# A hybrid decoder step: the projections of both branches as seven-product pairs in the stream

## The chip, the cores and the metric

The kernel runs on one core of one Trainium2 chip. The metric is the device time of one execution in microseconds (us). Engine names: PE is TensorE, DVE is VectorE, ACT is ScalarE, POOL is GpSimd, SP is SyncE, which issues nearly all DMAs.

## What is computed

One layer of a decoder trunk on 1024 prompt tokens, 16 learned meta tokens ahead of them, and 8 single decode tokens, with a model width of 1024. All data are float32.

```
xn   = rmsnorm(h, norm_pre)
proj = xn @ w_in                      # ten sections of 1024 columns
q, fr, i_in, z_a, b_g, c_g, h_c, z_b, gate_a, gate_b = split(proj)
o    = HGRN2 recurrence(silu(q), 1 - f, i_in, log f), per head    # f = lb + (1-lb)*sigmoid(fr)
y_a  = (headnorm(o) * silu(z_a)) @ w_a
y_b  = (b_g * conv3(c_g * h_c) * silu(z_b)) @ w_b
merged = sigmoid(gate_a) * y_a + sigmoid(gate_b) * y_b
out  = merged @ w_o
h    = h + rmsnorm(out, norm_post)
```

The recurrence is exact per token, and the new states of the recurrence and of the convolution are outputs too.

## The kernel before

Activations lie with channels on the partitions and tokens along the free axis, in two halves L and R of 516 or 524 columns (`HY`, `HL`; 512 prompt tokens and a few meta or decode tokens each). A product of float32 precision is made of three matmuls of rounded parts (`mm3`): high weight by high input, high by low, low by high. `split` makes such parts: ACT copies the high part, and DVE (or POOL) subtracts it from the value to give the low part.

**The stream** (`strassen`) computes the input projection. A pair is two output blocks of 128 channels for both halves of the tokens. Of the 2 x 2 blocks of the weights and the 2 x 2 blocks of the input it makes seven products instead of eight. The seven factor sets of the input (`b11`, `b21`, `t2`, `b12`, `t3`, `t4`, `b22`: tiles `s0h` to `s6l`) are made once at the start. Each product j has two steps (chunks of 256 columns and the rest), and each step four `mm3`, so 12 matmuls; a pair has 14 steps. In a step, after the matmuls, the work of the step before is flushed (the copy of a product out of PSUM into `sc`, which must come before the next product accumulates into the same bank; evacuations), then the high part of the weights of product i + 2 is made on ACT (first step) or its low part on DVE (second step). `load` fetches the weights of the next pair in the first three products; `add(p + 1)`, three POOL operations at j = 4, makes the sums of blocks of the next pair's weights; a fourth one (L615) follows within the next pair. All of this is in one order written out by hand (`manual_schedule`): each engine and SP's queue keep the order of the program, and semaphores hold them.

The stream has 39 pairs, numbered from 0: heads and gates up to pair 21, then `u_pair` and `b_pair` of the convolution in turns (pairs 22 to 37), and a last gate pair (38). `weave` puts other work between the steps: the recurrence `hgrn(m)` (42 steps a head), and then `sample_steps`, the decode tokens' recurrence, spread over 14*13 - 6 steps from step 350 on. Results wait in DRAM: `oz_d` (first branch), `ob_d` (second), `ga_d` and `gb_d` (gates).

**The projections of the branches** come after the stream. In its last pair (`tail`) the eight blocks of the first branch's input are loaded and split into the places of factor sets. `y_gemm` is called 16 times, for 8 output blocks of each branch: 8 blocks of input by 4 chunks by `mm3`, 96 matmuls. The gates are multiplied in at the evacuation, and the sum of both branches is `merged`, which stays on the chip. Then the output projection: `out_weight` and `merged_parts` split `w_o` and `merged` for k = 0 to 7, and `out_step` multiplies, 24 matmuls of 512 columns for each k of the first four token blocks.

All tiles of a tag named in `BUFS` have that many buffers, every other tag has one; a new tile of the same tag waits until the last reader of the old one is done, DMAs among them.

Of the kernel before, what the change touches and what calls it, by code (L numbers as in the profile page):

```python
# [19 lines left out]
HL = 524  # L20
HY = 516
# [11 lines left out]
def hybrid_step(ctx: ExitStack, tc: tile.TileContext,  # L33
# [122 lines left out]
    b11, b21, t2, b12, t3, t4, b22 = (factor(j) for j in range(7))  # L156
# [403 lines left out]
    def strassen(pairs, tail):  # L560
# [63 lines left out]
        for p, (_, chunks, _, evac, end) in enumerate(pairs):  # L624
# [3 lines left out]
            if p == len(pairs) - 1:  # L628
                tail["load"]()
            for j in range(7):  # L630
# [13 lines left out]
                for c, ((c0, n), pt) in enumerate(zip(chunks, dst)):  # L644
                    o = pt[:, 0:n]
                    for k in range(4):
                        xh, xl = at(factors[j], k)
                        mm3(o, w[:, 128 * k:128 * k + 128], w[:, 512 + 128 * k:640 + 128 * k],
                            xh[:, c0:c0 + n], xl[:, c0:c0 + n], k == 0 and not onto, k == 3, onto)
# [5 lines left out]
                    if c and p == len(pairs) - 1 and j in tail:  # L655
                        tail[j]()
# [18 lines left out]
    def u_pair(m):  # L675
# [55 lines left out]
        return (sec_of(5, m), sec_of(6, m)), chunks_of(518), (), evac, end  # L731

    def b_pair(m):
# [16 lines left out]
        return (sec_of(4, m), sec_of(7, m)), chunks_of(HY), (), evac, end  # L750

    def gate_pair(sec, m, dst):
# [9 lines left out]
        return (sec_of(sec, m), sec_of(sec, m + 1)), chunks_of(HY), (), evac, lambda: None  # L762

    def context_out():
        for g in range(2):
# [4 lines left out]
            nct = slot("sm", 512)  # L770
# [16 lines left out]
    def sample_steps():  # L787
        loaded = sample_state(0)
        for m in range(8):
# [43 lines left out]
    def place(tag, n, dt=F32R):  # L833

        t = slot(tag, n * NX, dt)
        return [t[:, NX * i:NX * i + NY] for i in range(n)]

    def one(*tags, dt=F32R):
        return [place(t, 1, dt)[0] for t in tags]

    RAWS = ("it", "u", "v", "a", "ee", "f", "k", "kt")

    def load_in(src, ks, tags):

        raws = {}
        for k in ks:
            raws[k] = slot(tags[k % len(tags)], NY)
            sync.dma_start(raws[k], src[k])  # L848
            if src is oz_d:
                pool.tensor_copy(cap(raws[k], 512, [[HY, 2], [1, 4]]), cap(smpz, 8 * k, [[4, 2], [1, 4]]))  # L850
        return raws

    def parts_of(raw, k, parts, hi, lo):
        split(raw[:, 0:NY], hi, lo)
        parts[k] = hi, lo

    def fill(src, parts, ks, places):
        raws = load_in(src, ks, RAWS[:5])
        for k, hi, lo in zip(ks, *places):
            parts_of(raws[k], k, parts, hi, lo)  # L860

    def in_factor(j):
        return place(f"s{j}h", 2), place(f"s{j}l", 2)

    pa, pb = {}, {}
    turn_in, homes = {}, {}

    def at_tail(ks):
        def go():
            for k in ks:  # L870
                if k not in homes:
                    his, los = in_factor(k // 2)
                    homes.update({k + i: (his[i], los[i]) for i in range(2)})
                parts_of(turn_in[k], k, pa, *homes[k])
        return go

    tail = {j: at_tail(ks) for j, ks in enumerate(((0,), (1, 2), (3, 4), (5,), (6,), (7,)))}
    tail["load"] = lambda: turn_in.update(load_in(oz_d, range(8), RAWS))

# [210 lines left out]
    merged = place("s4h", 2, F32) + place("s4l", 2, F32) + place("s5h", 2, F32) + place("s5l", 2, F32)  # L1090

    def y_gemm(w, parts, evac):
        wh, wl = w
        banks = [b() for b in ((hbank,) * 4 if y_gemm.n % 2 else (abank, abank, bbank, bbank))]
        y_gemm.n += 1
        for k in range(8):
            ks = slice(128 * k, 128 * k + 128)
            xh, xl = parts[k]
            for (h, c0, n), pt in zip(CH_Y, banks):
                o = HY * h + c0  # L1100
                mm3(pt[:, 0:n], wh[:, ks], wl[:, ks], xh[:, o:o + n], xl[:, o:o + n], k == 0, k == 7)
        for (h, c0, n), pt in zip(CH_Y, banks):
            evac(slice(HY * h + c0, HY * h + c0 + n), pt[:, 0:n])

    y_gemm.n = 0

    def gate_in(src, m):
        g = slot("x")
        sync.dma_start(g[:, 0:NY], src[m])
        return g  # L1110

    def w_y(w, m):
        return weight(w[0][:, 128 * m:128 * m + 128], lo=("f", "s")[m % 2])

    wa = w_y(w_a, 0)
    ga = gate_in(ga_d, 0)
    for m in range(8):
        w, g = wa, ga
        if m < 7:
            wa, ga = w_y(w_a, m + 1), gate_in(ga_d, m + 1)  # L1120
        else:
            wb, gb = w_y(w_b, 0), gate_in(gb_d, 0)
# [151 lines left out]
```

## Time and profile before

| | us |
|---|---|
| median of 3 runs (1290.95 to 1291.38) | 1290.95 |
| the profiled execution | 1289.68 |
| its span, first to last instruction | 1287.9 |
| PE busy | 1251.0 |
| DVE busy | 852.9 |
| ACT busy | 536.7 |
| POOL busy | 396.1 |

The profile is of one execution. Busy times are of instructions with their latency; matmuls overlap, so that the pace of PE is read from the starts of its instructions. A start is counted from the first instruction of the span. A release is inferred from semaphores.

### The profile page before, as it was taken

To read this page: it belongs to the slowest core of one execution; us is meant where nothing else is said; L and a number is where in the kernel's file an instruction comes from. 1 tells how busy PE (TensorE), PEld (TensorE's weight loads), DVE (VectorE), ACT (ScalarE), POOL (GpSimd) and SP (SyncE) were. 2 spreads that over 40 slices of the span, in tenths; PEclk is the share of its full clock that TensorE was granted. 3 is DMA by queue.
4 is the path that set the end of the run, shared out by engine and by line. 5 is a ranking of instruction groups with operands and counts; after the bars stand their busy time and mean duration, and the time that the engine had idled before them with its cause. 6 is when DMAs were issued, how large, how long until landed. Compare 5 with 4: busy or idle time off the path is not lost. (4 is left out here: it accounts for less than half of the span.)

```text
span 1287.9 us, 25281 instructions
## 1 busy us (share of the span) xinstructions
PE 1251.0 (97%) x10041; PEld 1216.1 (94%) x10041; DVE 852.9 (66%) x1444; ACT 536.7 (42%) x1280; POOL 396.1 (31%) x470
## 2 busy tenths in 40 slices
PE   6899999999999999999999999999999999999997
PEld 5799999999999999999999999999999999999876
DVE  5869597785968768596895776777768424446052
ACT  5555555555545455455443333333335312213031
POOL 5634232332423234232433454444543000000010
PEclk9899999999999999999999999999999999999999
DMA  7011212121221211222114415252428523432041
GB/s 224 9 36 58 69 58 84 52 75 51 68 69 58 83 53 58 61 67 74 53 42 133 124 58 157 75 156 58 124 91 310 178 85 106 156 99 99 2 166 58
DMA packets 146500, 117.11 MB, mean 91 GB/s; under 512 B 6641, under 2 KB 130650, under 8 KB 146382
## 3 DMA queue, kind: packets, MB, share of 16 engines
q1 hardware_dynamic: 145806, 113.40, 28.2%
q8 instruction: 79, 1.29, 0.4%
q0 software_dynamic: 576, 2.10, 0.4%
q14 instruction: 39, 0.32, 0.1%
HBM read 89.48 MB, written 25.96 MB: 90 GB/s over the span
## 5 line engine op out<-in xcount | busy, mean ns | idle before, releaser
L611 DVE TENSOR_TENSOR w<-wq,w 128x512 fp32r<-128x512 f32 x153 | 129.7, 847 | 57.7 <-ACT w L605 56.7
L605 ACT CAST w<-sm 128x512 fp32r<-128x512 f32 x117 | 72.4, 619 | 149.3 <-PE gb L116 123.3
L591 POOL TENSOR_TENSOR sm<-wq 128x512 f32<-128x512 f32 x39 | 67.1, 1721 | 166.1 <-DVE w L611 151.7
L570 ACT COPY sc<-ga 128x256 f32<-128x256 f32 x192 | 71.5, 373 | 105.1 <-PE ga L116 96.8
L611 DVE TENSOR_TENSOR w<-sm,w 128x512 fp32r<-128x512 f32 x117 | 87.0, 743 | 30.1 <-ACT w L605 29.6
L605 ACT CAST w<-wq 128x512 fp32r<-128x512 f32 x156 | 96.8, 621 | 14.5 <-PE ga L116 12.5
L114 PE MATMUL gb<-s1h,w 128*128 128x256 f32 (+3 forms) x344 | 99.2, 288 | 0.8 <-DVE sc L288 0.8
L615 POOL TENSOR_TENSOR sm<-wq,sm 128x512 f32<-128x512 f32 x39 | 60.3, 1545 | 123.1 <-DVE w L611 94.4
L115 PE MATMUL gb<-s1l,w 128*128 128x256 f32 (+3 forms) x344 | 96.8, 282 | 0.0
L114 PE MATMUL gb<-s3h,w 128*128 128x256 f32 (+3 forms) x328 | 94.6, 288 | 1.7 <-DVE sc L288 1.7
L114 PE MATMUL gb<-s6h,w 128*128 128x256 f32 (+3 forms) x328 | 94.5, 288 | 1.6 <-DVE f L288 1.6
L1187 POOL TENSOR_TENSOR st<-st,half 128x1 f32<-128x1 f32 (+1 forms) x9 | 5.0, 551 | 292.9 <-DVE st L1185 290.0
L115 PE MATMUL gb<-s3l,w 128*128 128x256 f32 (+3 forms) x328 | 92.5, 282 | 0.0
L115 PE MATMUL gb<-s6l,w 128*128 128x256 f32 (+3 forms) x328 | 92.4, 282 | 0.0
L116 PE MATMUL gb<-s3h,w 128*128 128x256 f32 (+3 forms) x312 | 88.4, 283 | 1.4 <-DVE w L611 1.2
L116 PE MATMUL gb<-s1h,w 128*128 128x256 f32 (+3 forms) x312 | 88.0, 282 | 0.5 <-DVE w L611 0.5
L116 PE MATMUL gb<-s6h,w 128*128 128x256 f32 (+3 forms) x312 | 88.1, 282 | 0.0
L114 PE MATMUL ga<-s0h,w 128*128 128x256 f32 (+3 forms) x288 | 83.2, 289 | 1.1 <-DVE zs L327 1.1
L115 PE MATMUL ga<-s0l,w 128*128 128x256 f32 (+3 forms) x288 | 81.2, 282 | 0.0
L114 PE MATMUL ga<-s2h,w 128*128 128x256 f32 (+3 forms) x272 | 79.8, 293 | 0.0
L288 DVE TENSOR_TENSOR sc<-gb,sc 128x256 f32<-128x256 f32 (+1 forms) x144 | 60.4, 421 | 27.1 <-PE gb L116 13.6
L593 POOL TENSOR_TENSOR sm<-wq 128x512 f32<-128x512 f32 x39 | 55.5, 1423 | 70.7 <-DVE w L611 67.9
(751 smaller groups left out, 4676.8 us busy)
## 6 DMA issues: line engine op xcount, KB each, us to landing
wq<-in_w_in_dram SPq DMA_DIRECT2D x160, 256.0 KB
oz<-zs SPq DMA_DIRECT2D x16, 258.0 KB
ob<-zs SPq DMA_DIRECT2D x8, 516.0 KB
x<-ga SPq DMA_DIRECT2D x8, 516.0 KB
x<-gb SPq DMA_DIRECT2D x8, 516.0 KB
wq<-in_w_a_dram SPq DMA_DIRECT2D x16, 256.0 KB
wq<-in_w_b_dram SPq DMA_DIRECT2D x16, 256.0 KB
wq<-in_w_o_dram SPq DMA_DIRECT2D x16, 256.0 KB
```

The source lines that it names most:

```text
L114: pe.matmul(pt, wh, xh, start=first, stop=False, skip_group_check=onto)
L115: pe.matmul(pt, wh, xl, start=False, stop=False, skip_group_check=onto)
L116: pe.matmul(pt, wl, xh, start=False, stop=last, skip_group_check=onto)
L288: vec.tensor_tensor(out=out, in0=pt, in1=s, op=ALU.add)
L570: act.copy(held[j][:, cols], o)
L591: pool.tensor_tensor(out=s3, in0=a11, in1=a21, op=ALU.subtract)
L593: pool.tensor_tensor(out=s2, in0=a21, in1=a11, op=ALU.subtract)
L605: act.copy(w[:, 0:512], source(i))
L611: (pool if j in pairs[p][2] else vec).tensor_tensor(out=w[:, 512:1024], in0=source(i), in1=w[:, 0:512].bitcast(F32), op=ALU.subtract)
L615: pool.tensor_tensor(out=s2, in0=raws[p, 0, 1], in1=s2, op=ALU.subtract)
L1187: pool.tensor_tensor(out=rs[0:rows], in0=rs[0:rows], in1=half[0:rows, 0:1], op=ALU.pow)
```

## The change

The projections of both branches become eight more pairs at the end of the stream (pairs 39 to 46, steps `A0` = 546 on; the second branch from `B0` = `A0` + 56). Each pair names its own factor sets (`sets`).

- `exchange` replaces the factor sets one by one: set j is filled anew after its last use in the pair before, in two units of 128 x 1032, by `split` (every third low part on POOL). Units come at steps base + 1 + 1.65 v, base being the start of the pair before the branch's first. Their raw blocks come from DRAM.
- The sums of blocks that some sets need are made by `block_sums`: load two blocks, four subtractions on POOL, write the two sums and the two others to DRAM (`t12`, `t34`). For the first branch it runs within `sample_steps` (m from 4 on), for the second (`b_sums`) at steps `A0` + 6 to `A0` + 31. The decode columns of the first branch are now written into `oz_d` by a DMA each.
- `sample_steps` is spread over 14*11 steps, with 20 steps of `block_sums` more in it.
- `y_pair` multiplies the gates at the evacuation; the first branch's result goes to DRAM (`md`) and is loaded again for the second.
- `context_out` moves from behind the stream to step `A0` + 2.
- The parts of the output projection for k = 0 to 2 are made in the last pair, the rest after it, each k in the place of a factor set. Tiles and banks of the output stage are named anew.

```diff
-        for p, (_, chunks, _, evac, end) in enumerate(pairs):
+        for p, (_, chunks, _, evac, end, sets) in enumerate(pairs):
...
-            if p == len(pairs) - 1:
-                tail["load"]()
...
-                        xh, xl = at(factors[j], k)
+                        xh, xl = at(sets[j], k)
...
-                    if c and p == len(pairs) - 1 and j in tail:
-                        tail[j]()
+                    for f in hooks.pop(14 * p + 2 * j + c, ()):
+                        f()
                     yield
...
+            sync.dma_start(oz_d[m][:].rearrange("p (h c) -> p h c", h=2)[:, :, 512:516],
+                           smpz[:, 8 * m:8 * m + 8].rearrange("p (h c) -> p h c", h=2))
             yield
+            if m >= 4:
+                yield from block_sums(m - 4, oz_d, *sums_a)
...
+    def block_sums(k, src, t12, t34):
+        up, low, t = slot("f", NY), slot("k", NY), slot("s", NY)
+        sync.dma_start(up, src[k])
+        sync.dma_start(low, src[k + 4])
+        yield
+        yield
+        less(t[:, L], up[:, R], up[:, L], pool)
+        less(t[:, R], low[:, R], t[:, L], pool)
+        yield
+        sync.dma_start(t12[k], t)
+        less(up[:, R], low[:, R], up[:, R], pool)
+        less(low[:, L], low[:, L], t[:, R], pool)
+        yield
+        sync.dma_start(t34[k][:, L], up[:, R])
+        sync.dma_start(t34[k][:, R], low[:, L])
+        yield
...
+    def exchange(g0, g1, base, sets, src, t12, t34, tags):
...
+        def load_unit(v):
+            if v < 14:
+                j, i = divmod(v, 2)
+                raw[v] = slot(tags[v % len(tags)], NY)
+                for q in range(2):
+                    sync.dma_start(raw[v][:, HY * q:HY * q + HY], of(j, 2 * i + q))
+
+        def unit(v):
+            j, i = divmod(v, 2)
+            if not i:
+                sets[j] = factor(j)
+            here = [[HL, 2], [1, HY]]
+            split(raw[v].rearrange("p (q c) -> p q c", q=2), cap(sets[j][0], 2 * HL * i, here),
+                  cap(sets[j][1], 2 * HL * i, here), pool if v % 3 == 2 else vec)
+            load_unit(v + len(tags))
+
+        for v in range(len(tags)):
+            at_step(g0 + int(g1 * v), lambda v=v: load_unit(v))
+        for v in range(14):
+            at_step(base + 1 + int(1.65 * v), lambda v=v: unit(v))
...
+    def y_pair(w, m, sets, second):
+        def evac(r, h, c0, n, pt, s):
+            ys = slice(HY * h + c0, HY * h + c0 + n)
+            g = gated_[second, m + r][:, ys]
+            vec.tensor_tensor(out=g, in0=added(pt, s), in1=g, op=ALU.mult)
+            if second:
+                t = merged[m + r][:, ys]
+                vec.tensor_tensor(out=t, in0=t, in1=g, op=ALU.add)
...
+    A0 = 14 * len(stream_of)
+    B0 = A0 + 56
...
+    exchange(A0 - 20, 1, A0 - 14, sets_a, oz_d, *sums_a, ("it", "u", "v", "a", "ee", "kt"))
+    exchange(B0 - 20, 1, B0 - 14, sets_b, ob_d, *sums_b, ("it", "u", "kt", "f", "k"))
+    at_step(A0 + 2, lambda: context_out())
+    b_sums = (x for k in range(4) for x in block_sums(k, ob_d, *sums_b))
+    for i in range(24):
+        at_step(A0 + 6 + int(1.25 * i), lambda: next(b_sums, None))
+    for i, m in enumerate((0, 2, 4, 6)):
+        at_step(A0 - 11 + 14 * i, lambda m=m: gates_in(ga_d, m))
+        at_step(B0 - 11 + 14 * i, lambda m=m: gates_in(gb_d, m))
+        at_step(B0 - 8 + 14 * i, lambda m=m: merged_in(m))
+    for k, g in enumerate((3, 6, 9)):
+        at_step(B0 + 42 + g, lambda k=k: (out_parts(k, 0), out_parts(k, 1)))
...
-    weave(stream, 14 * 13 - 6, sample_steps(), [1] * (8 * N_SAMPLE))
+    weave(stream, 14 * 11, sample_steps(), [1] * (8 * N_SAMPLE + 4 * 5))
     drain(stream)
-    context_out()
     ordered.close()
...
-        y_gemm(w, pa, lambda ys, pt: vec.tensor_tensor(out=merged[m][:, ys], in0=pt, in1=g[:, ys], op=ALU.mult))
...
-        y_gemm(w, pb, ev)
...
+    for k in (3, 4, 5):
+        out_parts(k, 0)
+        out_parts(k, 1)
+    for k, which in ((6, 1), (6, 0), (7, 1), (7, 0)):
+        out_parts(k, which)
```

## Rows read from the trace of the kernel before

**Rows 1.** The page: busy time, share of the span, instructions.

```profile
PE 1251.0 (97%) x10041; PEld 1216.1 (94%) x10041; DVE 852.9 (66%) x1444; ACT 536.7 (42%) x1280; POOL 396.1 (31%) x470
```

**Rows 2.** Windows: stretch, length, busy us by engine, granted clock, DMA share, GB/s.

```profile
700.00:980.00 280.00, 274.85 (x2358) 270.05 (x2358) 202.21 (x351) 101.61 (x235) 128.84 (x157) 1.00 0.39 121
980.00:1002.00 22.00, 21.42 (x178) 20.86 (x178) 19.95 (x27) 17.62 (x31) 3.01 (x5) 1.00 0.86 283
1002.00:1184.00 182.00, 182.00 (x1532) 182.00 (x1531) 75.05 (x160) 40.90 (x74) 0.00 (x0) 1.00 0.38 119
```

**Rows 3.** Timeline of PE: start, length in us, line, operands, columns.

```profile
979.94 0.28 PE L114 MATMUL ga<-s0h,w 128*128 128x256 f32 x1
982.78 0.28 PE L114 MATMUL gb<-s1h,w 128*128 128x256 f32 x1
...
1001.89 0.36 PE L114 MATMUL ga<-s0h,w 128*128 128x256 f32 x1
...
1184.71 0.40 PE L114 MATMUL ga<-s2h,it 128*128 128x512 f32 x1
```

**Rows 4.** Waits between 690 and 1000 us: total us, times, longest.

```profile
ACT w L605 <- POOL sm L591: 6.9, 3, 2.8
PE gb L114 <- DVE sc L288: 2.5, 2, 1.7
PE gb L116 <- DVE w L611: 1.7, 4, 0.5
```

**Rows 5.** Groups from 700 us on: busy us, mean ns, idle before.

```profile
L611 DVE TENSOR_TENSOR w<-wq,w 128x512 fp32r<-128x512 f32 x51 | 43.1, 845 | 6.9 <-ACT w L605 6.6
L288 DVE TENSOR_TENSOR sc<-gb,sc 128x256 f32<-128x256 f32 x19 | 7.9, 417 | 0.5 <-ACT sc L570 0.4
L91 DVE TENSOR_TENSOR s1l<-v,s1h 128x1032 fp32r<-128x1032 f32 x2 | 2.4, 1224 | 0.0
L91 DVE TENSOR_TENSOR f<-wq,w 128x512 fp32r<-128x512 f32 x16 | 10.3, 684 | 0.0
L605 ACT CAST w<-wq 128x512 fp32r<-128x512 f32 x54 | 33.6, 622 | 12.7 <-PE ga L116 10.8 <-issue 2.0
L570 ACT COPY sc<-ga 128x256 f32<-128x256 f32 x21 | 7.8, 373 | 12.5 <-PE ga L116 10.2 <-DVE w L611 2.3
L90 ACT CAST s1h<-v 128x1032 fp32r<-128x1032 f32 x2 | 2.1, 1054 | 0.1
```

**Rows 6.** The same groups on POOL, from 690 us on.

```profile
L615 POOL TENSOR_TENSOR sm<-wq,sm 128x512 f32<-128x512 f32 x14 | 23.1, 1650 | 49.9 <-DVE w L611 22.7 <-ACT w L605 12.5 <-ACT sc L570 7.1
L591 POOL TENSOR_TENSOR sm<-wq 128x512 f32<-128x512 f32 x13 | 22.1, 1702 | 32.1 <-DVE w L611 25.2 <-DMA wq<-in_w_in_dram 6.8
L593 POOL TENSOR_TENSOR sm<-wq 128x512 f32<-128x512 f32 x14 | 20.4, 1458 | 10.2 <-DVE w L611 7.5 <-DVE it L694 2.1
```

**Rows 7.** Timelines of DVE and POOL around 946 us: start, length.

```profile
946.42 1.22 DVE L804 TENSOR_TENSOR u<-u,v 128x1024 f32<-128x1024 f32 x1
...
946.59 2.21 POOL L591 TENSOR_TENSOR sm<-wq 128x512 f32<-128x512 f32 x1 [3.82 <-DVE w L611]
951.63 1.29 POOL L593 TENSOR_TENSOR sm<-wq 128x512 f32<-128x512 f32 x1 [1.13 <-DVE w L611]
```

**Rows 8.** A load in the chain, a wait for a small copy, DMA rate.

```profile
986.51 3.89 DMA it<-ob
...
DVE w L1235 <- DMA s<-w: 2.1, 1, 2.1
...
976.00:977.00 1.00, 1.00 (x11) 1.00 (x10) 1.00 (x2) 0.22 (x1) 1.00 (x1) 1.00 1.00 409
```

**Rows 9.** Windows near the start: columns as in rows 2.

```profile
48.00:50.00 2.00, 0.13 (x2) 0.00 (x0) 1.97 (x2) 0.59 (x1) 1.92 (x2) 1.00 0.00 0
50.00:52.00 2.00, 1.15 (x6) 1.18 (x7) 2.00 (x2) 0.03 (x1) 1.92 (x3) 0.53 0.04 8
56.00:58.00 2.00, 2.00 (x15) 1.84 (x14) 2.00 (x2) 0.34 (x1) 2.00 (x2) 0.77 0.02 4
```

More of the change, by code (lines that the diff above doesn't have):

```diff
@@ L841, in hybrid_step @@
[L841 to L877, printed above, removed]
@@ L878, in hybrid_step, with sums_of @@
-    tail["load"] = lambda: turn_in.update(load_in(oz_d, range(8), RAWS))
+            if m >= 4:
+                yield from block_sums(m - 4, oz_d, *sums_a)
+    def sums_of(name):
+        return [[kept.tile([128, NY], F32, name=f"{name}{i}{k}", tag=f"{name}{i}{k}") for k in range(4)] for i in range(2)]
+    sums_a, sums_b = sums_of("ta"), sums_of("tb")
+    L, R = slice(0, HY), slice(HY, NY)
+    def block_sums(k, src, t12, t34):
[14 more added lines that the diff above has]
+        yield
@@ new lines, in hybrid_step, with gates_in, merged_in, end @@
+    md = spilled("md")
+    gated_ = {}
+    merged = {}
+    MERGED = ("v", "a", "ee", "s", "it", "u", "kt", "f")
+    def gates_in(src, m):
+        for r, tag in ((0, "x"), (1, "zs")):
+            gated_[src is gb_d, m + r] = g = slot(tag, NY)
+            sync.dma_start(g, src[m + r])
+    def merged_in(m):
+        for r in range(2):
+            merged[m + r] = slot(MERGED[m + r], NY)
+            sync.dma_start(merged[m + r], md[m + r])
+    def y_pair(w, m, sets, second):
[6 more added lines that the diff above has]
+                vec.tensor_tensor(out=t, in0=t, in1=g, op=ALU.add)
+        def end():
+            if not second:
+                for r in range(2):
+                    sync.dma_start(md[m + r], gated_[second, m + r])
+        return (w[0][:, 128 * m:128 * m + 128], w[0][:, 128 * m + 128:128 * m + 256]), chunks_of(HY), (), evac, end, sets
@@ L880, in hybrid_step, with out_parts @@
+    homes = {}
+    def out_parts(k, which):
+        if k < 7:
+            if k not in homes:
+                homes[k] = factor(k)
+            hi, lo = (t[:, 1024 * which:1024 * which + 1024] for t in homes[k])
+        else:
+            hi, lo = (slot(t, 1024, F32R)[:, 0:1024] for t in ("x", "zs"))
+        (merged_parts if which else out_weight)(k, hi, lo)
     gates = [gate_pair(8, m, ga_d) for m in (0, 2, 4, 6)] + [gate_pair(9, m, gb_d) for m in (0, 2, 4, 6)]
@@ L1105, in hybrid_step @@
[L1105 to L1122, printed above, removed]
-        y_gemm(w, pa, lambda ys, pt: vec.tensor_tensor(out=merged[m][:, ys], in0=pt, in1=g[:, ys], op=ALU.mult))
-        if m == 1:
-            fill(ob_d, pb, (0, 1), in_factor(6))
-        if m == 3:
-            fill(ob_d, pb, (2, 3), (one("zs", "k"), one("zs", "kt")))
@@ L1152, in hybrid_step @@
-    for m in range(8):
-        w, g = wb, gb
-        if m < 7:
-            wb, gb = w_y(w_b, m + 1), gate_in(gb_d, m + 1)
-        def ev(ys, pt):
-            vec.tensor_tensor(out=g[:, ys], in0=pt, in1=g[:, ys], op=ALU.mult)
-            vec.tensor_tensor(out=merged[m][:, ys], in0=merged[m][:, ys], in1=g[:, ys], op=ALU.add)
-        y_gemm(w, pb, ev)
-        if m in (1, 2):
-            (h0, h1), (l0, l1) = in_factor(m + 1)
-            out_weight(2 * m - 2, h0, l0)
-            out_weight(2 * m - 1, h1, l1)
-        if m in (3, 4):
-            merged_parts(m - 3, *one(*(("it", "v"), ("a", "ee"))[m - 3]))
-        if m == 5:
-            merged_parts(2, *place("s4h", 2))
```

103 lines of the change are left out of this document (41 added, 62 removed).

## The prediction

> **What bounds the kernel now.** I read the busy shares first: TensorE (PE) is busy 97% of the span [rows 1]. Three stretches tell more [rows 2]: the u and b pairs with the sample steps beside them (700 to 980 us), the last pair of the stream (980 to 1002) and the two plain projections (1002 to 1184). In the last one PE has no gap and the granted clock is 1.00, while VectorE (DVE) works 75 of 182 us, ScalarE (ACT) 41 and GpSimd (POOL) not at all. So the projections are bound by PE's instruction count, with much room beside it. In the stretch before, DVE is at 72%, POOL at 46%, and PE loses 5 us of 280. Its waits name the operands of the next products and the emptying of PSUM [rows 4]. So in the seven-product form PE stays the bound, but what feeds it runs in order and close behind.
>
> **What the removed products are worth.** The plain projections run from 1001.89 to 1184.71 us [rows 3]: 182.8 us for 16 calls of 8 x 4 x 3 = 96 matmuls, 1536 in all, or 119.0 ns each. In seven-product form they are 8 pairs of 7 products of 2 x 4 x 3 = 24 matmuls, 1344 in all, with chunks of the same 256 and 260 columns. One product of the stream takes 982.78 - 979.94 = 2.84 us [rows 3], 118.3 ns a matmul, so the form changes the count and not the pace. I take 119.0 ns: 1344 of them are 159.9 us, **22.9 us less**, if PE never waits. A pair is then 20.0 us, and one of its 14 steps (12 matmuls) 1.43 us.
>
> The Trainium skill (TensorE: Matmul & The Clock Gate, Back-to-back issue gap) gives an isolated gap of columns / 2.4 + 2.5 ns, 110 ns for 258 columns; by it, as an estimate, the 192 matmuls would be worth 21.1 us. The trace shows 119 ns.
>
> **What is added, and what hides it.** Per pair DVE gets 7 low parts (0.68 us alone, 0.85 with POOL beside them), 6 additions and 8 multiplications of some 0.42 us, and in the second branch 8 additions more [rows 5]: 11 to 15 us of 20. ACT gets 7 high parts and 6 copies, 0.62 and 0.37 us [rows 5], 6.6 us. POOL gets four operations of block sums at 1.4 to 1.7 us [rows 6], some 6 us. All of that fits under 20 us of PE. Moving the context output costs nothing: its transposes are the same. The gates and the merged sums that go through DRAM are loaded a pair ahead.
>
> *Sums of blocks of the first branch* (in the sample steps, four times four subtractions on POOL) now stand in a stretch where POOL also carries the pairs' sums and half of u. Once, in pair 30, they come between the pair's sums and the last products of u, whose buffer the next pair's first copy wants. I count 1 us, between 0 and 4 (once in each of the four blocks). *The sample steps* are pressed from 176 steps into 154; the waits there were 2.5 and 1.7 us [rows 4], and I take 1 us more, between 0 and 4. Neither can be a gain: they add work and take room.
>
> *Sums of blocks of the second branch* (b_sums) are the step that matters. They are written into the steps 6 to 31 behind the first projection pair, 6.25 steps (8.9 us) for each of four blocks. Their three tiles (f, k, s) have one buffer each, so a block's loads wait until the previous block's results have been written to DRAM. POOL takes its instructions in order: while a subtraction waits for a load, the sums of the next pair's weights (add) wait behind it, ACT's cast of that sum waits in turn, and behind the cast on ACT the copy that frees the pair's first bank. Prices: a subtraction of 516 columns 1.29 us alone [rows 7] and 1.4 to 1.7 on average beside a busier DVE [rows 6]; I take 1.45, since DVE is less busy here. A load of 516 KB takes 3.9 us among others [rows 8], and alone 2.1 us (the small copy of the same rows) and 1.3 us of transfer at 409 GB/s, 3.4 us; a write of half as much is then 2.7 us. From the first projection pair's start, in us:
>
> - block 0: POOL is through with an exchange unit and L615 at about 6.2; a weight quarter waits for that on SP, and behind it stand two gate loads and the block's loads, issued at about 8.3, landed 13.0 behind those transfers; two subtractions to 15.9; the sums of pair 40 (3 x 1.45 and gaps) to 20.4; two subtractions to 23.3; written 26.0
> - block 1: landed 29.4; two to 32.3; the pair's second sum (L615) to 33.8; two to 36.7; written 39.4
> - block 2: landed 44.1 (behind two gate loads, 1.3 us more); four subtractions to 49.9; only then the sums of pair 41, which stand behind them in POOL's program, to 54.4
>
> The third product of pair 41 needs that sum, a cast (0.62) and a low part (0.75): 55.8 us. PE would be there after 32 steps, 45.8 us (0.3 later for L615 in block 1). It waits 9.7 us. After an almost idle stretch of PE the granted clock stood at 0.5 for about 6.8 us (from 0.53 in the stretch from 50 to 52 us and 0.77 in that from 56 to 58, PE busy 0.13 of 2 us ahead of it) [rows 9], the lower of the two levels (1.2 GHz), which costs 3.4 us of work at 2.4. Together 0.3 + 9.7 + 3.4 = **13.4 us**. With 1.29 us for a subtraction and no queue for the loads the wait is 4 us and the clock may hold; with 1.72 it is 15 us and the clock, 18.4 us. Bounds 4 and 18.4.
>
> *The exchanges in place*: 14 units of 128x1032, ten on DVE (1.22 us alone) and four on POOL (two times 1.29), with 1.05 us of ACT each [rows 5, 7]. A set is read last at step 2j+1 of its pair and wanted 13 steps later, while its two units come at about 3.3j+1 and 3.3j+2.7: the last has 4 steps, 5.7 us, to spare. At the first exchange DVE has 7 x 0.7 + 6 x 0.42 + 6 units = 15 us of 20; the pair that stood there before, with eight splits in it, lost 0.6 us as well between 980 and 1002 us [rows 2]. I take 0.5 us, between -0.6 and 3. At the second, over two pairs: 14 low parts at 0.8, ten units at 1.45 (between alone and the slow ones), 36 operations of 0.42 at the evacuations (28, and 8 additions of the second branch) take 41 us of 40. DVE falls behind; the operands have about two steps of slack. I take 2.5 us, between 0 and 8.
>
> *The last pair* has the splits of the output projection in it. Four casts (2.5 us) come on ACT between the two halves of the fifth product's copy, and the sixth product needs the second half: 1 to 3 us, I take 1.5. The output projection itself keeps its matmuls; its first three k are split by then, and each later k takes DVE some 3 us, while PE's 24 matmuls of it have twice a product's columns, so about twice its 2.84 us.
>
> **Sum:** -22.9 + 13.4 + 1 + 1 + 0.5 + 2.5 + 1.5 = -3.0 us. The profiled execution took 1289.68 us (span 1287.9) and lies 1.3 us under the median of 1290.95; the difference is taken to the median: **1288 us**.
>
> **Rivals.** *The block sums stay hidden* (chance 0.25). The copies and POOL run ahead of the order of the steps, since only semaphores hold them; if loads and writes return sooner than I took, or pair 41's sums get past, the 13.4 us shrink to 2 or less. For it: PE lost 5 us in 280 with POOL at 46%, and ACT waited for POOL's sums 6.9 us in three places, none over 2.8 us [rows 4]. Against it: 12 subtractions, 2 sums, three loads and two writes are one chain, and nothing overlaps in it. Time: 1290.95 - 22.9 + 6.5 = 1275, from 1272 to 1279.
>
> *DVE and POOL exclude each other, and the second exchange decides* (0.22, the other side). A POOL subtraction that started 0.17 us after a DVE operation with two SBUF inputs took 2.21 us, against 1.29 alone, while the DVE operation kept its 1.22 [rows 7]; DVE's low parts take 0.85 against 0.68 [rows 5]. If every such pair of operations is served one after the other, the two pairs of the second exchange hold 9.6 (low parts) + 12.2 (units) + 8.4 (20 multiplications and additions from SBUF) on DVE and 10.3 (pair sums) + 10.3 (units) on POOL: 51 us of work in 40. With some 3 to 4 us of slack PE then waits 7 us there, 2 at the first exchange (45 in 40), and the block sums go to their 1.72 us end: -22.9 + 18.4 + 2 + 2 + 7 + 1.5 = +8, 1299 us, from 1293 to 1304. It decides from where DVE's two-input operations and POOL's operations together pass the time of the pair.
>
> The Trainium skill (SBUF — State Buffer, SBUF: two separate sides) says the same as a rule: the port pair that DVE and GpSimd share is an exclusive lock for the whole instruction, and the loser fully blocks. The trace agrees in the instance above.
>
> *The count does not fall, or a product takes longer*: excluded by the pace of a product in the stream; 0.
>
> **How the numbers follow.** Forecast 0.53, with its own range of 1279 to 1296 (the block sums between their bounds, and a little for the small terms); hidden 0.25; port 0.22. A measurement of this kernel tells changes of about 0.2% (2.6 us) from none: faster means under 1288.4, slower over 1293.5. Of the forecast 0.29 lies below, 0.17 between and 0.07 above; of the port rival 0.21 is slower and 0.01 between. Faster 0.25 + 0.29 = 0.54, same 0.18, slower 0.28. The range leaves out the ends of the two rivals: 1274 to 1300.
>
> **What would show it.** PE's instructions fall by 192, and the stretch from the last gate pair to the output projection gets shorter than 182.8 us by what is left. The forecast is right if PE has one gap of 5 to 13 us in the third projection pair, released by a low part or copy behind POOL's sums, with POOL waiting for DMA before its subtractions and the granted clock at 0.5 behind the gap. If PE's longest wait there is under 2 us, the chain is wrong and the time is near 1275. If DVE is at 95% and more over the two pairs of the second exchange, with PE waiting for units or low parts, the port decides. Waits in the sample steps of over 8 us would make the small terms wrong.

## The result, and the profile after

The changed kernel takes **1312.08 us** (median of 4 runs, 1310.55 to 1312.5), the kernel before 1291.07 beside it: ratio **1.016, 95% interval 1.0143 to 1.0178**, slower by 21 us. The prediction was 1288, with a range of 1274 to 1300.

The page's first lines (busy us, share of the span, instructions) answer to [rows 1]:

```profile
span 1308.8 us, 25416 instructions
...
PE 1243.9 (95%) x9849; PEld 1203.7 (92%) x9849; DVE 940.0 (72%) x1520; ACT 578.3 (44%) x1364; POOL 504.7 (39%) x534
```

PE has 192 instructions less, as worked out, and yet a longer span: its idle time rose from 36.9 to 64.9 us. The windows cut the run at the first matmul of a pair (columns as in [rows 2]): pairs 25 to 37 (u and b pairs, sample steps), 38 (last gate pair, first exchange), 39 to 41 (first projection, b_sums), 42 to 44 (second exchange), 45 and 46.

```profile
702.37:990.64 288.27, 276.35 (x2338) 269.43 (x2337) 211.46 (x351) 101.96 (x235) 146.60 (x166) 1.00 0.46 140
990.64:1019.57 28.93, 22.90 (x170) 22.69 (x169) 16.27 (x20) 15.43 (x27) 10.93 (x6) 0.88 0.72 234
1019.57:1094.07 74.50, 65.35 (x514) 64.50 (x513) 49.11 (x68) 25.28 (x49) 43.40 (x29) 0.93 0.76 259
1094.07:1164.36 70.29, 63.76 (x507) 62.32 (x505) 63.69 (x88) 32.23 (x54) 31.66 (x18) 0.98 0.77 271
1164.36:1205.79 41.43, 41.43 (x343) 40.87 (x341) 35.55 (x74) 22.96 (x51) 6.49 (x5) 1.00 0.46 153
```

Against the kernel before (277.65 us for pairs 25 to 37, 21.95 for pair 38, 0.8 of it context output, that now stands in pair 39; 182.8 for the plain projections), and with 20.0 us for a pair that never waits (pair 45 took 20.1), the 21 us come out so: -22.8 arithmetic, +10.6 in pairs 25 to 37, +8.4 first exchange (7.8 in pair 38, 0.6 in pair 39), +13.1 in pairs 40 and 41, +10.3 second exchange (9.5 in pairs 42 and 43, 0.8 in 44), +1.4 in the last two. After the stream both kernels take 103 us.

**The chain of block sums** is there as written down. POOL's timeline (start, length, idle before):

```profile
1035.89 1.30 POOL L219 TENSOR_TENSOR s<-f 128x516 f32<-128x516 f32 x1 [4.07 <-DMA f<-ob]
...
1067.93 1.28 POOL L219 TENSOR_TENSOR s<-f 128x516 f32<-128x516 f32 x1 [8.38 <-DMA f<-ob]
1069.29 1.30 POOL L219 TENSOR_TENSOR s<-k,s 128x516 f32<-128x516 f32 x1
1070.56 1.27 POOL L219 TENSOR_TENSOR f<-k,f 128x516 f32<-128x516 f32 x1
1071.79 1.27 POOL L219 TENSOR_TENSOR k<-k,s 128x516 f32<-128x516 f32 x1
1073.02 1.26 POOL L591 TENSOR_TENSOR sm<-wq 128x512 f32<-128x512 f32 x1
1074.36 1.26 POOL L592 TENSOR_TENSOR wq<-wq 128x512 f32<-128x512 f32 x1
1075.69 1.26 POOL L593 TENSOR_TENSOR sm<-wq 128x512 f32<-128x512 f32 x1
```

Pair 41's sums end 57.4 us behind the start of pair 39 (54.4 was worked out). PE's wait of 7.1 us ends at 1077.93, in the third product of pair 41. The waits of PE and ACT show who stood behind them (us in total, times, longest):

```profile
PE h L114 <- ACT sc L570: 7.1, 1, 7.1
...
PE ga L114 <- ACT sc L570: 2.0, 1, 2.0
```

```profile
ACT w L605 <- POOL sm L593: 18.4, 2, 14.1
ACT w L605 <- POOL sm L615: 8.6, 2, 5.8
```

**The first exchange** has a wait that the prediction did not name. ACT's copy of PSUM into sc stands until a gate's two writes to DRAM have read that sc buffer (there are two buffers). ACT had the gate's halves ready at 998.57 and 1000.36; SP issued their writes at 1002.40 and 1004.44, behind loads of the exchange, and into queues that were full (DMA share 0.97 to 1.07 from 1002 to 1010 us). Of the second write's delay 4.1 us are SP's order and 6.3 us the time from issue to release. ACT's waits, SP's timeline, ACT's timeline, and windows of 2 us:

```profile
ACT sc L570 <- DMA gb<-sc: 6.9, 1, 6.9
```

```profile
1002.40 0.80 SPq L757 DMA_DIRECT2D gb<-sc  x1
1003.29 1.05 SPq L876 DMA_DIRECT2D v<-ta  x2
1004.44 0.39 SPq L757 DMA_DIRECT2D gb<-sc  x1
```

```profile
1010.78 0.37 ACT L570 COPY sc<-ga 128x256 f32<-128x256 f32 x1 [6.94 <-DMA gb<-sc]
```

```profile
1008.00:1010.00 2.00, 0.00 (x0) 0.00 (x0) 0.00 (x0) 0.00 (x0) 1.26 (x1) 1.00 1.07 400
1010.00:1012.00 2.00, 0.79 (x3) 0.79 (x4) 0.42 (x1) 1.22 (x2) 1.26 (x1) 0.51 0.98 373
1012.00:1014.00 2.00, 2.00 (x12) 2.00 (x11) 0.11 (x1) 2.00 (x5) 1.81 (x1) 0.50 0.12 44
```

PE and ACT idle, the DMA share at 1, and behind it the granted clock at 0.5, the level of 1.2 GHz, as near the start of the kernel before [rows 9]. Between 1000 and 1110 us it stood there for 20.4 us (from 1010.0, 1057.8, 1074.9 and 1105.6), each time late in a wait of PE or just behind one. PE worked for 16.2 us of that, at half the pace, so about 8 us of the excess are lost to it (an estimate).

**The second exchange** shows DVE and POOL by turns. Timeline of DVE, then of POOL:

```profile
1105.29 0.43 DVE L912 TENSOR_TENSOR x<-sc,x 128x260 f32<-128x260 f32 x1
...
1115.70 0.42 DVE L288 TENSOR_TENSOR sc<-gb,sc 128x260 f32<-128x260 f32 x1
1116.15 2.20 DVE L912 TENSOR_TENSOR zs<-sc,zs 128x260 f32<-128x260 f32 x1
1118.27 0.41 DVE L912 TENSOR_TENSOR zs<-ga,zs 128x256 f32<-128x256 f32 x1
...
1121.12 2.19 DVE L912 TENSOR_TENSOR x<-sc,x 128x256 f32<-128x256 f32 x1
```

```profile
1114.65 3.41 POOL L91 TENSOR_TENSOR s2l<-it,s2h 128x1032 fp32r<-128x1032 f32 x1
1119.76 3.26 POOL L91 TENSOR_TENSOR s4l<-f,s4h 128x1032 fp32r<-128x1032 f32 x1 [1.70 <-ACT s4h L90]
```

The multiplication of 260 columns took 0.43 us at 1105.29, where POOL was idle; [rows 7] had one meeting, in which POOL was the one that waited. At 1116.15 it took 2.20 and ended 0.3 us behind POOL's unit (1118.06); at 1121.12 it was the same. The sum at 1115.70, one operand in PSUM, took its 0.42 inside POOL's unit. The Trainium skill (SBUF — State Buffer, SBUF: two separate sides) has this distinction too: beside DVE's operations in a 2-port mode it names those with two SBUF inputs, against a GpSimd operation that reads SBUF. The trace agrees: in the groups from 1094 to 1144 us the multiplications of two SBUF operands average 874 to 1312 ns, the sums with one operand in PSUM 414 to 417.

```profile
L912 DVE TENSOR_TENSOR x<-sc,x 128x256 f32<-128x256 f32 x4 | 5.0, 1252 | 0.1
L912 DVE TENSOR_TENSOR x<-sc,x 128x260 f32<-128x260 f32 x4 | 3.5, 874 | 0.1
...
L288 DVE TENSOR_TENSOR sc<-gb,sc 128x260 f32<-128x260 f32 x6 | 2.5, 417 | 0.0
```

### The profile page after: what moved, and what is told of

It is laid out like the page before. It is cut to its first block, busy times and chain, and to the rows that moved or that the text cites. A ratio compares the mean times of both kernels' runs of the same rounds, so it can differ in the third digit from the quotient of the medians.

```text
span 1308.8 us, 25416 instructions
## 1 busy us (share of the span) xinstructions
PE 1243.9 (95%) x9849; PEld 1203.7 (92%) x9849; DVE 940.0 (72%) x1520; ACT 578.3 (44%) x1364; POOL 504.7 (39%) x534
## 5 line engine op out<-in xcount | busy, mean ns | idle before, releaser
L611 DVE TENSOR_TENSOR w<-wq,w 128x512 fp32r<-128x512 f32 x185 | 162.5, 878 | 66.3 <-ACT w L605 65.2
L611 DVE TENSOR_TENSOR w<-sm,w 128x512 fp32r<-128x512 f32 x141 | 112.4, 797 | 48.7 <-ACT w L605 48.2
L591 POOL TENSOR_TENSOR sm<-wq 128x512 f32<-128x512 f32 x47 | 79.0, 1680 | 172.3 <-DVE w L611 153.8
L605 ACT CAST w<-wq 128x512 fp32r<-128x512 f32 x188 | 116.7, 622 | 29.4 <-PE ga L116 21.4
L114 PE MATMUL gb<-s1h,w 128*128 128x256 f32 (+3 forms) x376 | 109.0, 290 | 2.0 <-DVE sc L696 1.8
L114 PE MATMUL gb<-s3h,w 128*128 128x256 f32 (+3 forms) x376 | 109.2, 291 | 1.6 <-ACT w L605 1.1
L116 PE MATMUL gb<-s3h,w 128*128 128x256 f32 (+3 forms) x376 | 107.4, 286 | 3.2 <-DVE w L611 3.1
L114 PE MATMUL gb<-s6h,w 128*128 128x256 f32 (+3 forms) x376 | 108.3, 288 | 2.3 <-DVE f L288 1.5
L116 PE MATMUL gb<-s1h,w 128*128 128x256 f32 (+3 forms) x376 | 106.3, 283 | 2.8 <-DVE w L611 2.8
L116 PE MATMUL gb<-s6h,w 128*128 128x256 f32 (+3 forms) x376 | 106.0, 282 | 0.0
L288 DVE TENSOR_TENSOR sc<-gb,sc 128x256 f32<-128x256 f32 x192 | 80.5, 420 | 35.2 <-ACT sc L570 18.1
L593 POOL TENSOR_TENSOR sm<-wq 128x512 f32<-128x512 f32 x47 | 65.3, 1389 | 74.6 <-DVE w L611 73.5
L114 PE MATMUL ga<-s5h,w 128*128 128x256 f32 (+3 forms) x288 | 85.3, 296 | 8.5 <-ACT sc L570 8.0
L115 PE MATMUL ga<-s5l,w 128*128 128x256 f32 (+3 forms) x288 | 83.3, 289 | 0.4 <-DVE s5l L200 0.4
```

Source lines behind the costliest of these rows:

```text
L114: pe.matmul(pt, wh, xh, start=first, stop=False, skip_group_check=onto)
L115: pe.matmul(pt, wh, xl, start=False, stop=False, skip_group_check=onto)
L116: pe.matmul(pt, wl, xh, start=False, stop=last, skip_group_check=onto)
L288: vec.tensor_tensor(out=out, in0=pt, in1=s, op=ALU.add)
L591: pool.tensor_tensor(out=s3, in0=a11, in1=a21, op=ALU.subtract)
L593: pool.tensor_tensor(out=s2, in0=a21, in1=a11, op=ALU.subtract)
```

## The experiments

All are edits of the changed kernel. Stage lengths in us, from the same marks in PE's timeline of one profiled execution each; the time is the median of the runs. Not every difference is an effect: pairs 42 to 44 take 69.2 to 70.6 us in the kernels whose edits leave the second branch's sums and both exchanges alone, pairs 39 to 41 take 74.5 to 77.4 without an edit of their own, and the kernel before, run beside each, had medians of 1289.3 to 1291.1.

| kernel | pairs 25-37 | 38 | 39-41 | 42-44 | time |
|---|---|---|---|---|---|
| changed | 288.3 | 28.9 | 74.5 | 70.3 | 1312.1 |
| samp176 | 292.1 | 29.1 | 76.4 | 69.8 | 1315.2 |
| aahead | 291.5 | 28.1 | 77.0 | 70.2 | 1316.9 |
| aphase | 295.5 | 29.0 | 76.8 | 69.2 | 1320.5 |
| asumtiny | 279.7 | 28.2 | 77.4 | 70.6 | 1304.6 |
| aheaddve | 282.0 | 29.1 | 77.4 | 70.6 | 1308.1 |
| gateaway | 287.6 | 20.4 | 82.9 | 70.2 | 1310.0 |
| gateaway2 | 290.9 | 20.4 | 81.1 | 70.0 | 1311.2 |
| bahead | 289.0 | 28.9 | 64.0 | 74.9 | 1305.0 |
| exdve | 288.1 | 29.1 | 74.4 | 66.1 | 1307.5 |
| comboB | 288.1 | 21.4 | 64.2 | 68.8 | 1293.1 |
| combo1 | 293.1 | 20.4 | 64.0 | 69.8 | 1296.8 |
| combo2 | 293.6 | 20.4 | 64.0 | 70.0 | 1297.7 |
| combo3 | 281.6 | 20.4 | 64.0 | 69.1 | 1284.6 |
| combo4 | 282.9 | 20.4 | 73.7 | 65.5 | 1291.6 |
| combo5 | 282.7 | 20.4 | 64.0 | 72.2 | 1289.4 |

### Pairs 25 to 37: room, loads, place, or POOL's work

samp176:

```diff
-    weave(stream, 14 * 11, sample_steps(), [1] * (8 * N_SAMPLE + 4 * 5))
+    weave(stream, 14 * 13 - 6, sample_steps(), [1] * (8 * N_SAMPLE + 4 * 5))
```

> The sample steps and the block sums of the first branch are woven over 176 steps of the stream again, as before the change, and not over 154; all else is as in the changed kernel. Theory A (room: the 108 small steps are pressed too close): pairs 25 to 37 fall from 288.3 us towards 279, the whole to about 1303 us. Theory B (POOL stands behind a load and a subtraction order, whatever the room): the waits only move, pairs 25 to 37 stay within 285 to 290, the whole 1308 to 1313 us. I hold B the likelier.

Room gives nothing back: 292.1 us, and 1315.2 for the whole, are over the ranges of both theories. The pressed sample steps are not the cause; B's "only moves" is nearer.

aahead:

```diff
-                yield from block_sums(m - 4, oz_d, *sums_a)
+                waiting.append(block_sums(m - 4, oz_d, *sums_a, ahead=3))
```

with a generator around sample_steps that takes one step of the waiting sums beside each step of the next sample, and again in 176 steps.

> The first branch's block sums run beside the next sample's steps and not between two samples: their loads are issued three small steps earlier before the first subtraction, and the whole has 176 steps of the stream again. Theory A (POOL stands at a subtraction whose load is under way, 7.2 us at 872, and what is queued behind it comes late): pairs 25 to 37 fall from 288.3 us (292.1 with 176 steps alone) to about 281, the whole to about 1305 us. Theory B (the 23 us of subtractions themselves on POOL are too much beside the pair's sums and u): they stay at 286 or more, the whole over 1309 us.

291.5 us. Theory A falls: pairs 31 and 33 do get shorter (from 26.0 and 27.9 to 23.9 and 24.8), but pairs 35 to 37 take 73.0 us and not 63.3. Against samp176 (292.1, also 176 steps) the new place is worth 0.6 us, which is within the spread.

aphase:

```diff
+    a_sums = [block_sums(k, oz_d, *sums_a) for k in range(4)]
+    for k, g in enumerate((14 * 32 + 12, 14 * 33 + 8, 14 * 34 + 12, 14 * 36 + 12)):
+        for i, s in enumerate((0, 2, 4, 7, 9, 10)):
+            at_step(g + s, lambda k=k: next(a_sums[k], None))
```

> The first branch's block sums, the same loads, subtractions and writes, are tied to steps of the pairs: they start at the end of a u pair (after its products have left) and end before the end of the next one, in the pairs 33, 33 to 34, 35 and 37; the 88 steps of the samples keep their 154 steps of the stream. Theory A (only where the subtractions fall matters: at the end of a u pair they stand ahead of u's products on POOL, which the convolution's taps on ACT wait for, and the casts of the weights stand behind these): pairs 31 and 33 fall from 26.0 and 27.9 to under 23 us, pairs 25 to 37 from 288.3 to some 280, the whole to about 1304 us. Theory B (their amount on POOL and in the DMA queues matters, wherever they stand): pairs 25 to 37 stay at 286 or more.

295.5 us (pairs 31 and 33 fall to 23.2 and 24.7, pairs 35 and 37 now take 30.6 and 27.2): the place is not the cause either. But the trace shows what the sums do. DVE's and POOL's timelines in pair 35:

```profile
931.53 1.24 DVE L722 TENSOR_SCALAR zs<-cx,vecs 128x8 f32<-128x8 f32 x1
932.81 1.33 DVE L723 SCALAR_TENSOR_TENSOR zs<-cx,vecs,zs 128x8 f32<-128x8 f32 x1
934.17 1.20 DVE L724 SCALAR_TENSOR_TENSOR zs<-x,vecs,zs 128x8 f32<-128x8 f32 x1
```

```profile
931.01 1.73 POOL L219 TENSOR_TENSOR s<-f 128x516 f32<-128x516 f32 x1
932.82 1.29 POOL L219 TENSOR_TENSOR s<-k,s 128x516 f32<-128x516 f32 x1
934.07 1.27 POOL L219 TENSOR_TENSOR f<-k,f 128x516 f32<-128x516 f32 x1
935.31 1.28 POOL L219 TENSOR_TENSOR k<-k,s 128x516 f32<-128x516 f32 x1
```

Three operations of 8 columns end with one POOL subtraction each, and two of them last as long as it does. The same kind takes 0.22 us in the changed kernel's groups:

```profile
L722 DVE TENSOR_SCALAR zs<-cx,vecs 128x8 f32<-128x8 f32 x7 | 1.5, 221 | 0.0
```

So POOL's work itself became the suspect.

asumtiny:

```diff
-        less(t[:, L], up[:, R], up[:, L], pool)
-        less(t[:, R], low[:, R], t[:, L], pool)
+        n = 8 if src is oz_d else HY
+        P, Q = slice(0, n), slice(HY, HY + n)
+        less(t[:, P], up[:, Q], up[:, P], pool)
+        less(t[:, Q], low[:, Q], t[:, P], pool)
```

and the other two alike, into t.

> The first branch's block sums subtract 8 columns of each half and not 516; their loads, writes and places in the order are as in the changed kernel (the first projection's sums of blocks are thereby left out of the computation, the blocks as loaded stand in their place). Theory A (the 23 us of POOL's subtractions, behind which POOL's other work and, at the port they share, DVE's operations with two SBUF operands come late): pairs 25 to 37 fall from 288.3 to 280 to 282 us, the whole to about 1305. Theory B (the loads, the small write of smpz and SP's order, which are all still there): 286 or more.

Theory A holds: with all loads and writes still there, 279.7 us, so 8.6 of the 10.6 us hang on POOL's subtractions. One thing goes with them: the writes no longer wait for the subtractions, for which SP, in order, had waited 21.7 us in the changed kernel (first line below). This run doesn't part the two; in aheaddve below, SP still waits for subtractions. POOL's busy time in the stretch falls from 146.60 to 125.66, DVE's from 211.46 to 203.40 with the same 351 operations:

```profile
SPq L851 <- POOL s L219: 21.7, 4, 6.8
```

```profile
703.06:982.75 279.69, 274.65 (x2338) 269.13 (x2337) 203.40 (x351) 102.17 (x235) 125.66 (x166) 1.00 0.47 145
```

aheaddve:

```diff
-        less(t[:, L], up[:, R], up[:, L], pool)
+        eng = vec if src is oz_d else pool
+        less(t[:, L], up[:, R], up[:, L], eng)
```

and the other three alike, run beside the next sample as in aahead, in 154 steps.

> The first branch's block sums on DVE, where a subtraction of two SBUF operands over 516 columns takes half of POOL's time, with the loads three small steps ahead, in the 154 steps of the changed kernel. Theory A (DVE and POOL take turns, so 10 us of DVE weigh less than 23 of POOL): pairs 25 to 37 fall from 288.3 to 281 to 284. Theory B (DVE's own load decides): 289 or more.

Theory A holds, 282.0 us: the same 16 subtractions cost 6.3 us less on the engine that is busier, and DVE's busy time does not rise (211.12 us, now for 367 operations). The place changed with the engine; by aahead against samp176 the place is worth 0.6 us of it. The whole falls by 4.0 us, since pairs 39 to 41 take 2.9 more, as in asumtiny.

```profile
703.40:985.39 281.99, 276.21 (x2338) 270.46 (x2337) 211.12 (x367) 101.75 (x235) 126.44 (x150) 0.99 0.46 143
```

### Pair 38: the gates' writes

gateaway:

```diff
+                if away and s is not None:
+                    if (r, h) not in outs:
+                        outs[r, h] = slot(("f", "k", "s")[r + h], HY)
+                    out = outs[r, h][:, c0:c0 + n]
```

> The last gate pair puts its gates into the free tiles f, k and s instead of back into the two sc buffers, so that the copies of PSUM into sc don't wait for the writes to DRAM. Theory A (the writes stand in SP's queue behind the exchange's loads and hold sc): pair 38 falls from 28.9 to some 21.5 us, the clock stays up at 1010 us, the whole to about 1304 us. Theory B (the exchange's units themselves, DVE and the full DMA queues hold the pair): ACT's wait goes, another takes its place, pair 38 stays at 27 us or more, the whole within 2 us of 1312.

Pair 38 falls to 20.4 us, so theory A holds for the pair: the writes are as late behind the pair's start as before (11.5 and 13.7 us; before 11.8 and 13.8), but the copies into sc no longer wait for them. But pairs 39 to 41 take 8.4 us more, and the sum stays. ACT's waits name a part of it:

```profile
ACT w L605 <- POOL sm L593: 23.6, 3, 16.6
...
ACT s L775 <- DMA gb<-s: 4.4, 1, 4.4
```

gateaway2:

```diff
-    at_step(A0 + 2, lambda: context_out())
+    at_step(A0 - 17, lambda: context_out())
```

> The last gate pair's gates in f, k and s as in gateaway, and the context output 19 steps of the stream earlier, so that its copies (tiles f and s) don't stand behind the gates' writes. Theory A (in gateaway the gain of 8.5 us was lost to ACT's 4.4 us wait of the context copy for a write, which this takes away): pair 38 stays at 20.4, pair 39 falls from 29.6 to 21 or 22, pairs 38 to 41 from 103.4 in the changed kernel to about 95 us, the whole to about 1304 us. Theory B (the loads of the block sums come no sooner, so that the chain behind pair 41 eats what is won): pairs 38 to 41 stay at 101 us or more, the whole 1309 us or more.

Pairs 38 to 41 take 101.5 us: theory B. The 4.4 us are gone, and the chain of block sums swallows the rest: POOL's sums for pair 41 end at 1077.6 (in the changed kernel 1077.0), though pair 39 began 5.5 us earlier. (Of pair 38's gain 0.9 us went to the context output, now in pair 37; pairs 25 to 37 took 2.6 us more in all, the rest without a cause shown.) What PE wins ahead of the chain, it waits for in it (9.3 us once, before 7.1):

```profile
PE h L114 <- ACT sc L570: 9.3, 1, 9.3
```

### Pairs 40 and 41: the block sums of the second branch

bahead, the generator cut to its core:

```diff
+            got[k] = [slot(t, NY) for t in (("f", "k", "s"), ("v", "a", "ee"))[k % 2]]
...
+            sync.dma_start(sums_b[1][k][:, L], up[:, R])
+            sync.dma_start(sums_b[1][k][:, R], low[:, L])
+            if k < 2:
+                loads(k + 2)
```

> The block sums of the second branch use two sets of tiles by turns (f, k, s and v, a, ee), each block's loads are issued a block ahead, and POOL's four subtractions of a block come in two places two small steps apart. Theory A (the chain of load, subtraction, write, load on one set of tiles stands on POOL before the pair's sums): POOL has no wait for DMA over 2 us there, PE's 7.1 us wait in pair 41 goes, pairs 40 and 41 fall from 53.1 to 41 or 42 us, the whole to about 1300 us. Theory B (it is the amount of POOL's work beside DVE): the two pairs fall by 4 us at most, the whole stays over 1307 us.

Theory A holds for the two pairs: they take 41.6 us, with the same 16 subtractions, and PE's longest wait there is 0.9 us. POOL no longer waits for the blocks' loads (its waits for other DMAs, up to 3.1 us, stay). But pair 39 takes 1.0 us more, and pairs 42 and 43 take 54.2, 4.7 more: the second exchange takes back part of the gain, so that the whole falls to 1305.0 and not to 1300.

```profile
PE ga L116 <- DVE w L611: 0.9, 1, 0.9
```

### Pairs 42 to 44: DVE's load, or turns with POOL

exdve:

```diff
-                  cap(sets[j][1], 2 * HL * i, here), pool if v % 3 == 2 else vec)
+                  cap(sets[j][1], 2 * HL * i, here), vec)
```

> All 14 units of each exchange have their low parts on DVE, none on POOL. Theory A (DVE and POOL exclude each other): in the two pairs of the second exchange POOL gives back 10.3 us and DVE takes 4.9 more, the work that can't overlap falls from 51 to some 45 us, pairs 42 and 43 fall from 49.5 to about 45 us, the whole to about 1306 us. Theory B (DVE's own load decides, POOL beside it is free): DVE has 46 us of work in 40, the two pairs take 53 us or more, the whole about 1315 us.

Theory A holds: pairs 42 and 43 fall from 49.5 to 45.3 us, and DVE, with more to do (57 operations against 54), is busy for less time (42.78 against 46.01 us). Some 1.7 of the 4.2 us are the clock, which no longer falls at 1105.6 (an estimate, half of its 3.4 us). First exdve, then the changed kernel:

```profile
1094.77:1140.05 45.28, 42.17 (x339) 40.72 (x338) 42.78 (x57) 25.85 (x40) 14.04 (x9) 1.00 0.93 330
```

```profile
1094.07:1143.57 49.50, 43.35 (x338) 42.11 (x337) 46.01 (x54) 25.74 (x40) 26.44 (x14) 0.97 0.87 309
```

### Together

comboB is gateaway2, bahead and exdve.

> Three edits together: gates in f, k, s with the earlier context output, the second branch's block sums on two sets of tiles, the exchanges' low parts all on DVE. Theory A (the three causes stand apart and their prices add: 8, 11.5 and 4.2 us): 1288 to 1290 us. Theory B (the second exchange is a bound of its own, and what is won ahead of it is given back there as in bahead, where pairs 42 and 43 took 4.7 us more): 1294 us or more, with pairs 42 and 43 at 50 us or more.

1293.1 us: between the two, nearer to theory A. 19 of the 23.7 us add up; pair 39 starts 7.3 us earlier than in the changed kernel, and with the chain gone that start is kept. Pairs 42 to 44 stay at 68.8. combo1 adds aahead, combo2 aphase:

> The three edits of comboB and the first branch's block sums as in aahead. If the prices add up, comboB's time less what aahead wins (some 7 us if POOL's wait for the loads was the cause): about 1282 us, faster than before. If aahead wins nothing, this is within 2 us of comboB.

> comboB's three edits and the first branch's block sums placed as in aphase. By theory A of aphase 1293.1 - 8 = about 1285 us, 0.3% faster than before; by theory B 1292 to 1295 us, slower than before.

Neither helped (1296.8 and 1297.7 us, 3.7 and 4.6 over comboB), in line with aahead and aphase alone. combo3 has comboB's edits and aheaddve's.

> comboB (1293.1 us) with the first branch's block sums as in aheaddve. By theory A of aheaddve 1286 to 1289 us; by B 1294 or more.

**1284.6 us, ratio to the kernel before 0.9958 (0.9943 to 0.9974)**: the change with these four edits is faster than the kernel before, by 5.4 us. The second exchange still costs some 9 us (69.1 for three pairs of 20.0). combo4 moves the sums of the weights too:

```diff
-                pool.tensor_tensor(out=s3, in0=a11, in1=a21, op=ALU.subtract)
+                eng = vec if p > 41 else pool
+                eng.tensor_tensor(out=s3, in0=a11, in1=a21, op=ALU.subtract)
```

and the other three operations alike.

> combo3 with the sums of the weights' blocks (three of four operations for the pairs from 42 on, the fourth from 41 on) on DVE as well, so that POOL is idle in the second exchange. Theory A (taking turns at the port): 4 operations of 1.3 us on POOL become 4 of 0.7 on DVE, some 2.5 us a pair less of work that can't overlap, pairs 42 to 44 fall from comboB's 68.8 to some 64 us, 4 to 5 us under combo3. Theory B (DVE's load): 2.7 us more DVE work a pair, 71 us or more, slower than combo3.

Pairs 42 to 44 fall to 65.5 us, near theory A's 64, but pair 41 loses 9.7, and the whole is 7.0 us over combo3 and not 4 to 5 under it. DVE, in order, now stands behind the load of a weight quarter where POOL stood before. Pairs 42 and 43 in combo3, then in combo4:

```profile
1068.83:1116.52 47.69, 44.18 (x339) 42.22 (x337) 40.21 (x56) 25.31 (x40) 14.89 (x10) 0.96 1.01 358
```

```profile
1080.44:1125.23 44.79, 42.27 (x338) 41.87 (x337) 40.39 (x65) 25.66 (x40) 0.00 (x0) 0.96 0.90 314
```

That turns at the port made the gain is not shown. PE's wait in pair 41 may give the second exchange a head start: behind such a wait pairs 42 to 44 are shorter in other kernels too, 66.1 us in exdve against 68.8 without it in comboB, 70.3 in the changed kernel against 74.9 in bahead. And with POOL idle the two pairs still take 4.8 us more than 40, with the clock at 0.96: turns are not all that bounds them. combo5 begins one pair later (p > 42):

> combo4 with the weights' sums on DVE one pair later (from pair 43 on, the fourth operation from pair 42 on). In combo4 the first of them put DVE behind a weight quarter that was still under way (5.5 us at 1074), PE then waited 7.15 us. Theory A (turns at the port in the second exchange, and that one wait apart): pair 41 falls from 29.8 to 20.1, pairs 42 to 44 stay at 65 to 66 us where combo3 has 69.1, the whole 1280 to 1282 us. Theory B (DVE meets such a load in every pair once PE gets ahead): another wait of DVE for a weight quarter, pairs 41 to 44 at 89 us or more, the whole at or over combo3's 1284.6.

Theory B: the wait comes again, a pair later, and DVE's timeline shows it:

```profile
1089.32 0.69 DVE L592 TENSOR_TENSOR sm<-wq 128x512 f32<-128x512 f32 x1
1094.10 0.69 DVE L593 TENSOR_TENSOR wq<-wq 128x512 f32<-128x512 f32 x1 [4.08 <-DMA wq<-in_w_b_dram]
```

Pair 42 takes 30.5 us, pairs 43 and 44, behind that wait, 21.1 and 20.6 (combo3: 23.0 and 21.4). The whole, 1289.4 us, is 4.8 over combo3.

## Why the prediction was wrong, point by point

The sum missed by 24 us, in three terms that stood too low: the first branch's block sums (by 8.6), the first exchange (7.9) and the second (7.8). In each the prediction looked at one engine's work or at PE's old waits, and not at what the added work holds up on other engines.

- **Arithmetic, -22.9 us: right.** The stream kept 20.0 us a pair where nothing waits (pair 45 took 20.1).
- **Block sums of the second branch, 13.4 us: right in mechanism, and in size partly by luck.** 13.1 us, but 4.0 of them in pair 40, where 0.3 was reckoned, and 9.1 in pair 41, where it was 13.1. bahead won 11.5 of them with the same subtractions, so it is the chain and not the work. The blocks' first subtractions came 16.3, 31.2 and 48.4 us behind pair 39's start where the loads were reckoned to land at 13.0, 29.4 and 44.1, so the sums of pair 41 were 3 us late; PE, itself late by pairs 39 and 40, waited no more for it.
- **Block sums of the first branch and compressed sample steps, 1 + 1 us: wrong, 10.6.** The step counted the sums as 1 us for one meeting, in pair 30, and priced the pressed sample steps by PE's waits of before (2.5 and 1.7 us), as if POOL's 46% were room. Most of the loss fell in pairs 31 and 33 (5.2 and 4.3 us more than before). asumtiny shows 8.6 us for the subtractions, samp176 that the room was no part of it. DVE at 72% and POOL at 46% were not room: where both read SBUF they take turns. How much of the 8.6 us is turns, how much POOL's own order (its sums for the next weights behind four subtractions) and how much SP's waits for the subtractions, no run separates. 2 us of the 10.6 stay without a cause shown.
- **First exchange, 0.5 us: wrong, 8.4.** The prediction summed DVE's work (15 of 20 us) and did not look at who holds sc: the exchange's loads stood on SP ahead of the gates' writes and filled the queues that these went into. The bounds, -0.6 to 3, were taken from the pair that stood there before, which had its loads in other places. gateaway shows the cause; gateaway2 shows that the term could not be won alone, as the chain behind it ends at a time that PE does not set.
- **Second exchange, 2.5 us of 0 to 8: wrong, 10.3.** DVE's load was summed alone (41 of 40 us). The port rival's sum, 51 us, is near the 49.5 us that the two pairs took, and its 45 after exdve's edit near the 45.3. But the sum is no bound to the microsecond: with the same work the pairs took 54.2 us in bahead, and with exdve's 46.6 in comboB and 47.7 in combo3. That rival was right in its place and its mechanism, and near with its 7 us of waits (6.6 us of PE's waits from 1094 to 1145 us were ended by low parts and sums of DVE; of the rest of the 10.3 some 1.7 are the clock, an estimate, and 2 are not accounted for). Its time, 1299, was 13 us short all the same.
- **Last pair, 1.5 us: right in size**, 1.3; no run tests its mechanism.

What was wrong over all is that forecast and port rival stood as alternatives: the forecast had the 13 us of the chain and a small exchange, the rival the exchange and a longer chain, and both mechanisms ran beside each other, with a third, the writes behind SP's order and full queues, in neither. The marks of the prediction told it: a gap of 7.1 us in the third projection pair behind POOL's sums, DVE busy for 46.0 of 49.5 us (93%, the mark was 95%) in the second exchange, and PE idle for 11.9 us beside the sample steps (5 in the kernel before).

## What to carry to other kernels

Where DVE and POOL both work on SBUF operands, add the times that those operations take alone, on both engines, and compare the sum with the stretch. Busy shares don't serve for it: they hold waiting and operations from PSUM, and in the kernel before DVE and POOL were busy for 331 of 280 us together [rows 2] while PE lost 5. The sum is a guide and not the time. Subtractions given to the "idle" POOL cost more than the same ones on DVE. For every DMA that is moved, list what it is now ahead of on its queue, and which buffer each delayed write still holds. A chain that starts with a load ends when it ends: what is won ahead of it is waited for at its end, so the chain is to be broken first (another set of tiles, loads a block ahead), and an engine that takes over work also takes over its waits for loads.

## What the runs showed of the hardware

- A DVE operation with SBUF operands alone, even of 8 columns, can last until the POOL operation it meets is done: 0.22 us became 1.20 to 1.33 (8 columns), 0.43 became 2.20; with one operand in PSUM 0.42 stayed 0.42. DVE's busy share counts that waiting as work.
- With the DMA engines at a share of 1.07 (400 GB/s) a write of 260 columns, issued at 1004.44 us, held its source tile until 1010.78, 6.3 us.
- The granted clock stood at 0.50 (1.2 GHz) for 6.8 us from within PE's long waits of 6.0 and 7.1 us (from 1010.0 and 1074.9; PE started again at 1011.2 and 1077.9), and for 3.4 us from just behind the shorter ones of 2.0 and 1.9 us (from 1057.8 and 1105.6; PE had started again at 1057.6 and 1105.0). In combo3's stretch of pairs 39 to 41, without such waits, it is 1.00.
